# Shifting the moving tiles of a transformer block's matmuls by unused gaps in SBUF

## The chip, the cores and the metric

The kernel runs on one core of a Trainium2 chip. The metric is device time of one launch in microseconds; before the change the median of three runs is 1527.2 us. Everything said about single instructions comes from one profiled execution of the program.

## The reference

One encoder layer on 256 tokens of width 2048, in float32, with 256 memory tokens:

```python
h = rms_norm(x, norm_g[l, 0])
q, k, v, g, lr, u_f, u_h, u_s = jnp.split(h @ w_in[l], split_at, axis=-1)
...                                   # four mixers: gated linear attention, FFT, long and short convolution
x = x + mix @ w_out[l]
x = x + cross_attention(rms_norm(x, norm_g[l, 1]), mem_n, w_xq[l], w_xkv[l], w_xo[l])
x = x + swiglu(rms_norm(x, norm_g[l, 2]), w_gate_up[l], w_down[l])
return rms_norm(x, final_norm_g)
```

`cross_attention` has 4 heads of width 512: queries from the tokens, keys and values from the memory, softmax, output projection. `swiglu` is `(silu(h @ w_gate) * (h @ w_up)) @ w_down` with an inner width of 5632, which is 44 tiles of 128.

## The kernel before

Activations are held transposed: one tile `[128, 512]` per 128 features, with the high part of the 256 tokens in columns 0 to 255 and the low part (what the rounding to the matmul's type left over) in columns 256 to 511. Such tiles are `act0` to `act23`, `oex0` to `oex3` (attention output), `pt0` and `pt1` (transposed probabilities), `q`, `kt` (queries and transposed keys of a head) and `f0` to `f35` (SwiGLU). Values are kept as `vh` and `vl`, high and low part in tiles of their own.

All weights stream through the class `Stream`: `Stream._half` (L89, L90) takes 1024 columns of a loaded slab `raw`, casts them into `wh` on ScalarE and subtracts into `wl` on VectorE. There are three buffers of each, and up to the end of the attention one more pair from an extra pool. `Block.mm` (L262 to 272) multiplies one 128 x 128 block of weights, stationary, with one activation tile, moving: `wh` with all 512 columns (L269), `wl` with the 256 high columns (L270). That is a pair. In narrow places the first is split into two of 256 columns (L266, L267). `Block.gemm` runs `mm` over the reduction tiles `k` of each output column, one column after the other, except for a first group of four columns that are interleaved by parts. `gemm_rows` (L321 to L323) does it the other way round: activations stationary, weights moving.

The order of the stages in time: keys and values of the memory, the input projection with the four mixers, the output projection of the mixers, the queries of four heads with scores and probability-value products between them (`attention` and `head`), the attention's output projection, gate and up of the SwiGLU, down of the SwiGLU, the final norm. The queue of small steps between matmuls (`Background`) is filled while the program is recorded, by estimated costs of matmuls and VectorE work, and not by addresses.

`attention` opens three pools: `atp` for `oex`, `pt` and the scale `qs`; `kp` for `kt`, `q`, `vh`, `vl`; `mp` with five buffers `mr`, into which keys and values come back from DRAM through POOL's queue (L580). The output projection's moving tiles are

```python
o = act[0:8] + oex + act[8:12]
```

and in `mlp` the down projection's are

```python
f = act[4:12] + [fp.tile([P, 512], F32R, name=f"f{i}") for i in range(36)]
```

so 8 of its 44 reduction tiles are `act` tiles and 36 are `f` tiles. In `head`, `kt` moves over the stationary `q` (L637, L638), and `pt` over the stationary `vh` and `vl` (L664, L665).

Pools are laid out one behind the other in a partition, so the size of what lies ahead of a tile sets its address. The start addresses in bytes of a partition, as the built programs have them, and their remainders modulo 512 (all tiles of a kind have the same remainder, and so have all 128-column blocks of a weight tile):

| tiles | before | remainder | after | remainder |
|---|---|---|---|---|
| `act0`.. (moving) | 16512.. | 128 | 16512.. | 128 |
| `wh`, `wl` (stationary) | 128224.. | 224 | 128224.. | 224 |
| `f0`.. (moving over `wh`, `wl`) | 152800.. | 224 | 153216.. | 128 |
| `oex0`.. (moving over `wh`, `wl`) | 160992.. | 224 | 161408.. | 128 |
| `pt0`.. (moving over `vh`, `vl`) | 169184.. | 224 | 169600.. | 128 |
| `kt` (moving over `q`) | 173312.. | 256 | 173824.. | 256 |
| `q` (stationary) | 189696.. | 256 | 190304.. | 352 |
| `vh`, `vl` (stationary) | 206080.. | 256 | 207072.. | 224 |
| `mr` (landing place) | 222464.. | 256 | 223456.. | 224 |

Moving less stationary, modulo 512, is 416 for `act` over the weights in both programs; for `f` and `oex` over the weights 0 before and 416 after; for `kt` over `q` 0 and 416; for `pt` over `vh` and `vl` 480 and 416.

Of the kernel before, what the change touches and what calls it, by code (L numbers as in the profile page):

```python
# [13 lines left out]
F32 = mybir.dt.float32  # L14
F32R = mybir.dt.float32r
# [7 lines left out]
P = 128  # L23
# [126 lines left out]
class Block:  # L150
# [42 lines left out]
    def split2(self, hi, lo, src):  # L193
        self.nc.scalar.copy(hi, src)
        self.tt(lo, src, hi.bitcast(F32), ALU.subtract)

    def sumsq(self, acc, src, first):
        if first:
            self.nc.scalar.activation(acc, src, AF.Square)
        else:  # L200
            s = self.tmp()
            self.nc.scalar.activation(s, src, AF.Square)
            self.tt(acc, acc, s, ALU.add)
# [343 lines left out]
    def attention(self):  # L547
        tc, nc, act, st = self.tc, self.nc, self.act, self.st
        with tc.tile_pool(name="atp", bufs=1) as atp, tc.tile_pool(name="kp", bufs=1) as kp, \
                tc.tile_pool(name="mp", bufs=5) as mp:  # L550
            oex = [atp.tile([P, 512], F32R, name=f"oex{i}") for i in range(4)]
            pt = [atp.tile([P, 512], F32R, name=f"pt{i}") for i in range(2)]
            qs = atp.tile([P, 2], F32, name="qs")
            o = act[0:8] + oex + act[8:12]
            slot = lambda name, n: kp.tile([P, 512], F32R, name=name, tag=name, bufs=n)
            kv = [([], [], []) for _ in range(4)]

            def ev_q(q, p):
                q.append(slot("q", 8))
                self.split(q[-1], self.merge(p))  # L560

            def scales():

                col = self.rstd_begin([[self.acc]], D)
                nc.vector.tensor_scalar(out=qs, in0=col, scalar1=512 ** -0.5, scalar2=None, op0=ALU.mult)
                yield

            heads = []

            def load_kv():  # L570

                todo = [(hd, what, i) for hd in range(4) for what in range(2) for i in range(4)]
                parts = []

                def fetch():
                    if len(parts) < len(todo):
                        hd, what, i = todo[len(parts)]
                        m = mp.tile([P, R], F32, name="mr", tag="mr")
                        o = (4 * hd + i) * R
                        nc.gpsimd.dma_start(m, (self.vd if what else self.kd)[:, o:o + R])  # L580
                        parts.append(m)

                for _ in range(5):
                    fetch()
                yield 4
                for n, (hd, what, i) in enumerate(todo):
                    while hd > len(heads) + 1:
                        yield
                    if what == 0:
                        kv[hd][0].append(slot("kt", 8))  # L590
                        self.split(kv[hd][0][-1], parts[n])
                    else:
                        if i % 2 == 0:
                            kv[hd][1].append(slot("vh", 4))
                            kv[hd][2].append(slot("vl", 4))
                        c = slice(i % 2 * R, i % 2 * R + R)
                        self.split2(kv[hd][1][-1][:, c], kv[hd][2][-1][:, c], parts[n])
                    fetch()
                    yield 1.0

            def scores(hd, q):
                while len(kv[hd][2]) < 2:
                    yield
                yield
                yield from self.head(q, *kv[hd], pt, o[4 * hd:4 * hd + 4], qs)
                heads.append(hd)

            lp = [list(range(8)), list(range(8, 16))]
            self.bg.add(scales())
            self.bg.add(load_kv())  # L610
            gens = []
            for hd in range(4):
                q = []
                if hd > 1:
                    self.bg.drain(gens[hd - 2], True)
                self.gemm("w_xq", [(4 * hd + i) * P for i in range(4)], self.h2, lambda i, p: ev_q(q, p), first=(4, lp),
                          before=lambda n: n and hd == 0 and self.bg.drain(self.late))
                gens.append(self.bg.add(scores(hd, q)))
            h3 = self.h3 = act[12:24] + act[0:4]

            def ev_o(i, p):
                self.residual(i, p, V_NG + 32 + i, h3[i] if i < 12 else None)
                if i == 12:
                    st.extra = None

            self.gemm("w_xo", [i * P for i in range(16)], o,
                      ev_o,
                      first=(4, [list(range(12)), list(range(12, 16))]), before=lambda n: n == 1 and self.bg.drain())
            self.bg.add(self.rest(h3, 12, V_NG + 32))
# [41 lines left out]
    def mlp(self):  # L671
        tc, nc, act = self.tc, self.nc, self.act
        with tc.tile_pool(name="fp", bufs=1) as fp:
            f = act[4:12] + [fp.tile([P, 512], F32R, name=f"f{i}") for i in range(36)]
            box = {}

            def ev(i, p):
                u = self.merge(p)
                self.tt(u, u, box["rs"], ALU.mult)
                if i % 2 == 0:  # L680
                    nc.scalar.activation(u, u, AF.Silu)
                    box["g"] = u
                else:
                    self.tt(u, u, box["g"], ALU.mult)
                    self.split(f[i // 2], u)

            cols = []
            for j in range(FT):
                cols += [j * P, DFF + j * P]
            self.bg.add(self.rstd_later(self.acc, D, box))  # L690
            self.gemm("w_gate_up", cols, self.h3, ev, first=(4, [list(range(12)), list(range(12, 16))]),
                      before=lambda n: n and self.bg.drain())
            warm = self.tmp()[:, 0:1]
            nc.scalar.activation(warm, self.ones[:, 0:1], AF.Sqrt)
            last = self.tmp()

            def ev_down(i, p):
                x = self.resk(i)
                self.tt(x, x, p[:, 0:R] if i == 15 else self.merge(p), ALU.add)
                sq = last if i == 15 else self.acc if i == 0 else self.tmp()  # L700
                nc.scalar.activation(sq, x, AF.Square)
                if 0 < i < 15:
                    self.tt(self.acc, self.acc, sq, ALU.add)
                nc.scalar.activation(x, x, AF.Copy, scale=self.gvec(V_FG, i))

            self.gemm("w_down", [i * P for i in range(16)], f, ev_down,
                      first=(4, [list(range(40)), list(range(40, 44))]), narrow_last=True)

            p = self.bank()[:, 0:R]
            for i, a in enumerate((self.acc, last)):  # L710
                nc.tensor.matmul(p, self.ones, a, start=i == 0, stop=i == 1)
            v, y, a, rs = (self.tmp() for _ in range(4))
            nc.vector.tensor_scalar(out=v, in0=p, scalar1=1.0 / D, scalar2=EPS, op0=ALU.mult, op1=ALU.add)
            nc.scalar.activation(a, v, AF.Sqrt)
            nc.vector.reciprocal(y, a)
            self.stt(a, y, -0.5, y, ALU.mult, ALU.mult)
            self.tt(a, a, v, ALU.mult)
            self.stt(p, a, 1.5, y, ALU.add, ALU.mult)
            nc.scalar.copy(rs, p)
            for i in range(0, KT, 2):  # L720
                x = self.res[i // 4][:, i % 4:i % 4 + 2, :]
                if i in POOLS:
                    nc.gpsimd.tensor_tensor(out=x, in0=x, in1=rs.unsqueeze(1).to_broadcast([P, 2, R]), op=ALU.mult)
                else:
                    self.tt(x, x, p.unsqueeze(1).to_broadcast([P, 2, R]), ALU.mult)
                (nc.scalar if i % 4 else nc.sync).dma_start(self.t["out"][:, i * R:(i + 2) * R], x.rearrange("p k r -> p (k r)"))
# [513 lines left out]
```

## Time and profile before

| | |
|---|---|
| median of three runs | 1527.2 us (1527.15 to 1528.36) |
| the profiled execution | 1526.68 us, of which its span 1524.6 us |
| PE (matmul) busy | 1502.2 us, 99% of the span |
| VectorE, ScalarE busy | 995.5 us, 787.3 us |
| granted TensorE clock, mean | 0.995 |
| attention's output projection | about 679 to 772 us |
| gate and up | about 772 to 1262 us |
| down | about 1264 to 1509 us |

[...] A row of a group reads: line, engine, operation, written tile, read tiles (moving first, then stationary), shapes, count; busy time of the group and mean duration of one in ns; idle time of the engine ahead of it and what ended most of that. In the table of stages each row is a stretch in us, its length, and for PE, PEld, DVE, ACT and POOL the busy time and the number of instructions, then the granted clock, the share of the DMA engines and GB/s.

### The profile page before, as it was taken

To read this page: it belongs to the slowest core of one execution; us is meant where nothing else is said; L and a number is where in the kernel's file an instruction comes from. 1 tells how busy PE (TensorE), PEld (TensorE's weight loads), DVE (VectorE), ACT (ScalarE), POOL (GpSimd) and SP (SyncE) were. 2 spreads that over 40 slices of the span, in tenths; PEclk is the share of its full clock that TensorE was granted. 3 is DMA by queue.
4 is the path that set the end of the run, shared out by engine and by line. 5 is a ranking of instruction groups with operands and counts; after the bars stand their busy time and mean duration, and the time that the engine had idled before them with its cause. 6 is when DMAs were issued, how large, how long until landed. Compare 5 with 4: busy or idle time off the path is not lost.

```text
span 1524.6 us, 22257 instructions
## 1 busy us (share of the span) xinstructions
PE 1502.2 (99%) x8788; PEld 1311.2 (86%) x8788; DVE 995.5 (65%) x1532; ACT 787.3 (52%) x1238; POOL 40.0 (3%) x76
## 2 busy tenths in 40 slices
PE   8999999999999999999999999999999999999996
PEld 7887788889999788888888888888888888888885
DVE  6676668678667766867766666666666664555454
ACT  6664555557445655656554444444444444444442
POOL 0100100000002000100000000000000000000000
PEclk9999999999999999999999999999999999999998
DMA  9965554354346555544545555555555555555552
GB/s 353 343 239 190 198 193 166 139 195 159 139 167 241 195 190 182 177 149 166 194 166 193 189 185 185 189 192 194 193 193 186 186 186 190 192 192 180 183 191 83
DMA packets 48808, 290.53 MB, mean 191 GB/s; under 512 B 6173, under 2 KB 7486, under 8 KB 17088
## 3 DMA queue, kind: packets, MB, share of 16 engines
q1 hardware_dynamic: 44912, 279.59, 51.5%
q0 software_dynamic: 3072, 8.39, 1.6%
q8 instruction: 69, 1.13, 0.3%
q10 hardware_dynamic: 720, 1.13, 0.2%
q14 instruction: 35, 0.29, 0.0%
HBM read 282.80 MB, written 6.29 MB: 190 GB/s over the span
## 4 chain that ended last, share of the span: by engine, by line
PE 96%; DVE 1%; DMA 1%; issue 1%; ACT 0%; SPq 0%; POOL 0%; DVEq 0%; POOLq 0%; ACTq 0%
PE pg L269 49%; PE pg L270 28%; PE pg L266 3%; PE pg L267 3%; PE pg L321 3%; PE pg L323 2%; PE pg L322 2%; PE pm L269 1%; PE pm L796 1%; DMA mr<-values 1%; PE pm L664 1%; PE pm L270 0%; PE pm L637 0%; DMA raw<-in_W 0%; DVE wl L90 0%
## 5 line engine op out<-in xcount | busy, mean ns | idle before, releaser
L269 PE MATMUL pg<-act,wh 128*128 128x512 f32 x2680 | 939.7, 394 | 8.3 <-DVE act L182 4.5
L90 DVE TENSOR_TENSOR wl<-raw,wh 128x1024 fp32r<-128x1024 f32 (+1 forms) x507 | 617.0, 1218 | 425.9 <-ACT wh L89 423.6
L270 PE MATMUL pg<-act,wl 128*128 128x256 f32 x3008 | 842.5, 281 | 0.0
L89 ACT CAST wh<-raw 128x1024 fp32r<-128x1024 f32 (+1 forms) x507 | 529.5, 1046 | 589.5 <-PE pg L269 333.4
L269 PEld LDWEIGHTS pg<-act,wh 128*128 128x128 f32 x2680 | 504.7, 188 | 120.7 <-ACT wh L89 4.5
L270 PEld LDWEIGHTS pg<-act,wl 128*128 128x128 f32 x3008 | 566.9, 189 | 2.6 <-issue 2.0
L269 PE MATMUL pg<-f,wh 128*128 128x512 f32 x540 | 191.3, 398 | 0.0
L270 PE MATMUL pg<-f,wl 128*128 128x256 f32 x576 | 161.8, 281 | 0.0
L269 PEld LDWEIGHTS pg<-f,wh 128*128 128x128 f32 x540 | 101.5, 188 | 25.2
L270 PEld LDWEIGHTS pg<-f,wl 128*128 128x128 f32 x576 | 108.8, 189 | 0.0
L266 PE MATMUL pg<-act,wh 128*128 128x256 f32 x328 | 94.8, 289 | 0.0
L267 PE MATMUL pg<-act,wh 128*128 128x256 f32 x328 | 92.1, 281 | 0.0
L178 DVE TENSOR_TENSOR tmp<-pg,tmp 128x256 f32<-128x256 f32 x183 | 76.2, 417 | 5.7 <-ACT tmp L276 5.0
L276 ACT COPY tmp<-pg 128x256 f32<-128x256 f32 x179 | 65.0, 364 | 14.6 <-PE pg L270 14.5
L321 PE MATMUL pg<-wh,act 128*128 128x512 f32 x160 | 66.4, 415 | 0.0
L323 PE MATMUL pg<-wh,act 128*128 128x512 f32 x160 | 63.3, 395 | 0.0
L322 PE MATMUL pg<-wl,act 128*128 128x512 f32 x160 | 62.9, 393 | 0.0
L266 PEld LDWEIGHTS pg<-act,wh 128*128 128x128 f32 x328 | 61.9, 189 | 0.7
L267 PEld LDWEIGHTS pg<-act,wh 128*128 128x128 f32 x328 | 61.9, 189 | 0.3
L178 DVE TENSOR_TENSOR tmp<-tmp,rs 128x256 f32<-128x256 f32 x88 | 37.3, 425 | 2.9
L321 PEld LDWEIGHTS pg<-wh,act 128*128 128x128 f32 x160 | 30.0, 188 | 10.4 <-issue 2.9
L322 PEld LDWEIGHTS pg<-wl,act 128*128 128x128 f32 x160 | 30.1, 188 | 7.5 <-issue 1.0
(233 smaller groups left out, 985.1 us busy)
## 6 DMA issues: line engine op xcount, KB each, us to landing
raw<-in_W SPq DMA_DIRECT2D x247, 1024.0 KB, 4.8
raw<-in_W SPq DMA_DIRECT2D x9, 512.0 KB, 7.3
res<-in_xT SPq DMA_DIRECT2D x8, 512.0 KB, 5.6
k<-in_mem SPq DMA_DIRECT2D x8, 256.0 KB, 9.0
k<-in_x SPq DMA_DIRECT2D x8, 256.0 KB, 8.2
keys<-tmp POOLq DMA_DIRECT2D x16, 128.0 KB, 5.7
values<-tmp POOLq DMA_DIRECT2D x16, 128.0 KB, 2.4
mr<-keys POOLq DMA_DIRECT2D x16, 128.0 KB, 3.5
```

Of the source, the lines that this page charges most:

```text
L89: nc.scalar.copy(wh[:, a:b], r[:, a:b])
L90: nc.vector.tensor_tensor(out=wl[:, a:b], in0=r[:, a:b], in1=wh[:, a:b].bitcast(F32), op=ALU.subtract)
L178: self.nc.vector.tensor_tensor(out=out, in0=a, in1=b, op=op)
L266: self.nc.tensor.matmul(p[:, 0:R], wh, slot[:, 0:R], start=start, stop=False)
L267: self.nc.tensor.matmul(p[:, 0:R], wh, slot[:, R:512], start=False, stop=False)
L269: self.nc.tensor.matmul(p[:, :], wh, slot[:, :], start=start, stop=False)
L270: self.nc.tensor.matmul(p[:, 0:R], wl, slot[:, 0:R], start=False, stop=stop)
L276: self.nc.scalar.copy(t, p[:, R:512])
L321: nc.tensor.matmul(ps[r][:, :], hi, wh, start=k == 0, stop=False)
L322: nc.tensor.matmul(ps[r][:, :], hi, wl, start=False, stop=False)
L323: nc.tensor.matmul(ps[r][:, :], lo, wh, start=False, stop=k == nk - 1)
L664: nc.tensor.matmul(p[:, :], vh[m][:, s], pt[m][:, :], start=m == 0, stop=False)
```

## The change

Unused tiles ("gaps") go ahead of `oex`, `q`, `vh` and `f` in their pools, `q` and the values get pools of their own, and `qs` grows from 8 to 128 bytes, of which the instructions still use 8.

```diff
+    def gap(self, pool, n):
+
+        pool.tile([P, n // 4], F32, name=f"gap{next(self.kept)}")
...
         with tc.tile_pool(name="atp", bufs=1) as atp, tc.tile_pool(name="kp", bufs=1) as kp, \
+                tc.tile_pool(name="qp", bufs=1) as qp, tc.tile_pool(name="vp", bufs=1) as vp, \
                 tc.tile_pool(name="mp", bufs=5) as mp:
+            self.gap(atp, 416)
+            self.gap(qp, 96)
+            self.gap(vp, 384)
             oex = [atp.tile([P, 512], F32R, name=f"oex{i}") for i in range(4)]
             pt = [atp.tile([P, 512], F32R, name=f"pt{i}") for i in range(2)]
-            qs = atp.tile([P, 2], F32, name="qs")
+            qs = atp.tile([P, 32], F32, name="qs")[:, 0:2]
             o = act[0:8] + oex + act[8:12]
-            slot = lambda name, n: kp.tile([P, 512], F32R, name=name, tag=name, bufs=n)
+            slot = lambda name, n: dict(kt=kp, q=qp).get(name, vp).tile([P, 512], F32R, name=name, tag=name, bufs=n)
...
         with tc.tile_pool(name="fp", bufs=1) as fp:
+            self.gap(fp, 416)
             f = act[4:12] + [fp.tile([P, 512], F32R, name=f"f{i}") for i in range(36)]
```

## The prediction

> **What bounds the kernel now.** I read the page first, then the stages one by one, then the starts of single matmuls. Part 1 of the page, the chain that ended last and two rows of part 5:
>
> ```profile
> span 1524.6 us, 22257 instructions
> ...
> PE 1502.2 (99%) x8788; PEld 1311.2 (86%) x8788; DVE 995.5 (65%) x1532; ACT 787.3 (52%) x1238; POOL 40.0 (3%) x76
> ...
> PE 96%; DVE 1%; DMA 1%; issue 1%; ACT 0%; SPq 0%; POOL 0%; DVEq 0%; POOLq 0%; ACTq 0%
> ...
> L269 PE MATMUL pg<-act,wh 128*128 128x512 f32 x2680 | 939.7, 394 | 8.3 <-DVE act L182 4.5
> ...
> L269 PE MATMUL pg<-f,wh 128*128 128x512 f32 x540 | 191.3, 398 | 0.0
> ```
>
> TensorE is on 96% of the chain, so a nanosecond more or less on a matmul arrives at the end of the kernel. The last two rows are the same instruction on two kinds of moving tile, and `f` costs 4 ns more by the modelled durations. The starts say it better, because matmuls overlap. The table of stages, restricted to TensorE's stretches in the SwiGLU (gate and up, then down):
>
> ```profile
> 772.00:1262.00 490.00, 489.98 (x2828) 431.24 (x2828) 318.51 (x456) 238.30 (x356) 0.00 (x0) 1.00 0.53 189
> 1262.00:1512.00 250.00, 248.93 (x1455) 217.94 (x1454) 123.90 (x136) 109.86 (x138) 0.00 (x0) 1.00 0.48 173
> ```
>
> The second number is PE busy. In gate and up, 2828 matmuls are 1414 pairs (`wh` with 512 columns, `wl` with 256) in 490.0 us: 346.5 ns a pair, all of them on `act` tiles. The clock is 1.00 in both stages, VectorE is busy 65% and 50%. Now one output column of the down projection, which goes through 8 `act` tiles and then 36 `f` tiles; start, duration, instruction:
>
> ```profile
> 1400.94 0.39 PE L269 MATMUL pg<-act,wh 128*128 128x512 f32 x1
> ...
> 1403.72 0.40 PE L269 MATMUL pg<-f,wh 128*128 128x512 f32 x1
> ...
> 1416.42 0.39 PE L269 MATMUL pg<-act,wh 128*128 128x512 f32 x1
> ```
>
> Eight pairs on `act` take 2.78 us, 347 ns each; 36 pairs on `f` take 12.70 us, 353 ns each. Same stage, same weights, same shapes, no waits. One by one the `f` pairs repeat 350, 361, 349 ns from start to start; the `act` pairs stand at 346 to 348 within two or three pairs after them. What differs is the address of the moving tile. `act` lies at remainder 128 modulo 512 and the weights `wh`, `wl` at 224, so `act` is 416 bytes past them; `f` lies at 224, 0 past. The output projection of the attention reads 12 `act` and 4 `oex` tiles (`oex` also at 224), and the scores read `kt` over `q`, both at 256:
>
> ```profile
> L269 PE MATMUL pg<-act,wh 128*128 128x512 f32 x186 | 65.5, 393 | 0.0
> ...
> L269 PE MATMUL pg<-oex,wh 128*128 128x512 f32 x64 | 23.3, 398 | 0.0
> ...
> L637 PE MATMUL pm<-kt,q 128*128 128x512 f32 x8 | 2.9, 398 | 0.0
> ```
>
> That is the group view from 679 to 772 us. `oex` pairs are at 350 to 361 ns where `act` pairs are at 347, and the last head's scores show the same cycle of 350, 361, 349. So wherever the moving tile lies 0 past the stationary one, the cycle can appear; heads 0 and 1 of the scores, also at 0, settle at 347, so 0 allows the slow cycle rather than forces it.
>
> **The change part by part.** In the built programs each engine issues the same instructions in the same order with the same semaphore waits; only addresses differ, and the row length of `qs`. Nothing is added to an engine or a queue. After the change `f`, `oex` and `pt` lie at 128, `q` at 352, `vh`, `vl` and `mr` at 224; `kt` stays at 256. Every pair of moving and stationary is then 416 apart, except the projections that hold `act` stationary and stream the weights (96, untouched).
>
> *`f`, down projection.* The 540 pairs exceed 346.8 ns each by 3.3 us together (15 columns of 12.70 - 36 x 0.3468 = 0.215 us give 3.2). The nearest row for what they become is `act` in the same columns, at the same remainder: 346.8 ns. Bounds: 346 and 361 ns, the fastest and the slowest pair seen, so from 3.7 us saved to 4.4 us lost (540 x 8.2 ns); I take 346.8, as 1409 pairs in gate and up average that. The last column is narrow, three matmuls of 256 columns a tile: 108 steps at 119.9 ns on `f` against 118.75 on `act`, 0.1 us.
>
> *`oex`.* 63 measured pairs exceed 346.8 by 0.3 us, and the `act` pairs that follow them, which carry the cycle for a few pairs, by another 0.25. Together 0.55 us.
>
> *Scores and `pt`.* 64 pairs. The scores exceed 346.8 ns by about 0.1 us without their waits; the probability-value product (480 apart today) has mostly 347 and some 361, 0.1 us. Some of the latter sits beside waits of PE for `pt`, so I count 0.15, with ends 0 and 0.25.
>
> *`qs`, the gaps.* A gap tile is never written. `qs` grows from 2 to 32 columns, but the instructions still touch 2. Casts and subtractions into `f` write at 128 instead of 224; the casts take 406 ns into `act` (at 128) and 399 into `f` (at 224), the subtractions 418 into both, and PE waits for neither in this stage, so nothing.
>
> *What would be late next.* The down projection takes a half slab of weights per 8 pairs: 2.78 us instead of 2.82. The supply needs 1.05 us of ScalarE and 1.22 of VectorE per half, and gate and up already runs at 2.77 with more evacuation beside it. So it holds.
>
> Sum: 3.3 + 0.1 + 0.55 + 0.15 = 4.1 us. The profiled execution took 1526.68 us, of which the span is 1524.62; it lies 0.5 us below the median of the runs, 1527.2. It would become 1522.6, and the median 1523.1.
>
> [...]
>
> **The rivals.** *It is the place, not the offset.* `act` lies at bytes 16,512 to 65,664 of a partition, the weights at 128,224 to 160,992, `f` and `oex` from 152,800 up. If high tiles are slow to stream, shifting them by 416 bytes changes nothing: 1527.2. For it: no high tile at 416 exists in this trace. Against it: `pt`, from 169,184, streams mostly at 347 ns a pair at offset 480, and heads 0 and 1 of the scores, from 173,312, at 347, while `oex` beside `pt` cycles.
>
> *The change does not do what it says.* It does: the addresses above are those of the changed program. What stays open is only whether they matter.
>
> *Slower: the fetch of keys and values.* PE's longest stop after the start is here:
>
> ```profile
> 498.94 0.79 PE L269 MATMUL pg<-act,wh 128*128 128x512 f32 x1 [3.73 <-DVE tmp L178]
> ```
> ```profile
> 495.94 0.40 ACT L194 CAST vh<-mr 128x256 fp32r<-128x256 f32 x1 [3.02 <-DMA mr<-values]
> ```
> ```profile
> 499.00:504.50 5.50, 5.50 (x17) 0.51 0.73 262
> ```
>
> ScalarE stands 3.02 us before the cast of `vh` until the transfer into `mr` lands, the next weight cast stands behind it, and PE idles 3.73 us. The granted clock is then 0.51 for 5.5 us: seven pairs at 0.64 us instead of 0.347, 2.05 us more. The `mr` tiles move from remainder 256 to 224. Two landings of 4.6 us lie on the chain before the stop. If they lengthened, PE would stop longer by twice that. To end slower than before by over 0.2% they must lengthen by (4.1 + 3.05) / 2 = 3.6 us each, 78%, giving 1530.3 or more. Against: `raw` already lands at remainder 224 and takes 1024 KB in 4.8 us. The same place can also move the other way: two landings shorter by 1 us each give 2 us and, if the clock then stays up, another 2.05: about 1519.
>
> **How the numbers follow.** The 4.1 us saved: 0.79. No effect of the offset: 0.12. Slower by the fetch: 0.05. The stop at 498.94 shortens as well: 0.04. 0.2% of the time, about what a measurement of this kernel can tell from no change, is 3.05 us, so the forecast clears it by 1.0 us; the three runs lie 1.2 us apart, and I give a tenth of the first case to "within". Faster 0.79 x 0.9 + 0.04 = 0.75; same 0.08 + 0.12 = 0.20; slower 0.05. The likeliest case alone spans 1522.2 to 1524.4. The range reaches down to a slightly shorter stop, 1521.4, and up towards the case without effect, 1526.6.
>
> **What would show it.** Right: in the changed profile the `f` row reads 392 ns like `act` in that stage, one column of 36 `f` pairs takes 12.48 us instead of 12.70, the down projection's PE stretch is 3.4 us shorter, gate and up and everything before 476 us is unchanged, and `oex` is at 347 ns a pair. Wrong: the `f` pairs still cycle through 350, 361, 349 (the place decides), or the difference sits around 480 to 505 us (the fetch decides). If `f` is at 347 and the time hardly moves, the stop at 498.94 has grown.

## The result, and the profile after

| | before | after |
|---|---|---|
| median of nine runs each | 1527.79 us (1526.0 to 1528.36) | 1523.4 us (1521.86 to 1524.58) |
| the profiled execution | 1526.68 us, span 1524.6 | 1523.47 us, span 1521.4 |

The ratio of after to before is 0.9971, with a 95% interval of 0.9961 to 0.9982: 4.4 us less, by more than the 0.2% that can be told from no change. A later series of eight runs gave 0.9973 (0.9962 to 0.9983).

The page of the changed kernel, part 1 and the two rows of part 5 that stood in the prediction. The diff shifts the lines of the file, so L269 is now L273 and L270 is L274:

```profile
span 1521.4 us, 22257 instructions
...
PE 1498.4 (98%) x8788; PEld 1310.7 (86%) x8788; DVE 995.8 (65%) x1532; ACT 787.3 (52%) x1238; POOL 40.0 (3%) x76
...
L273 PE MATMUL pg<-act,wh 128*128 128x512 f32 x2680 | 939.6, 394 | 9.3 <-ACT wh L89 4.9
...
L273 PE MATMUL pg<-f,wh 128*128 128x512 f32 x540 | 187.9, 392 | 0.0
```

The `act` row is what it was; the `f` row fell from 398 to 392 ns. PE busy fell by 3.8 us. By stages (stretch, length, then busy us and count for PE, PEld, VectorE, ScalarE and POOL, then clock, DMA share, GB/s):

```profile
772.00:1262.00 490.00, 489.98 (x2827) 431.24 (x2827) 319.23 (x457) 237.97 (x355) 0.00 (x0) 1.00 0.54 189
1262.00:1512.00 250.00, 245.74 (x1458) 217.56 (x1457) 126.61 (x140) 110.56 (x138) 0.00 (x0) 1.00 0.49 173
```

Gate and up is unchanged to one matmul; the down projection has 245.7 us of work where it had 248.9. The same kind of output column as before, 8 `act` tiles and then 36 `f` tiles:

```profile
1399.44 0.39 PE L273 MATMUL pg<-act,wh 128*128 128x512 f32 x1
...
1402.21 0.39 PE L273 MATMUL pg<-f,wh 128*128 128x512 f32 x1
...
1414.69 0.39 PE L273 MATMUL pg<-act,wh 128*128 128x512 f32 x1
```

The 36 `f` pairs take 12.48 us, 346.7 ns each, where they took 12.70. The two matmuls of a pair last 0.39 and 0.28 us in the profile, 0.67 together, so they overlap, and the starts are what is compared. From start to start all 540 `f` pairs of the trace are at 346 or 347 ns; the cycle of 350, 361 and 349 is gone. In the attention's output projection the groups now read

```profile
L273 PE MATMUL pg<-act,wh 128*128 128x512 f32 x191 | 66.9, 392 | 0.0
...
L273 PE MATMUL pg<-oex,wh 128*128 128x512 f32 x60 | 21.7, 393 | 0.0
```

where `oex` stood at 398. One row went the other way. The stop of PE near 499 us is longer than before, 4.42 us instead of 3.73, with ScalarE standing before a cast of `vh` as before and with the same slow clock after it:

```profile
500.21 0.79 PE L273 MATMUL pg<-act,wh 128*128 128x512 f32 x1 [4.42 <-DVE tmp L178]
```
```profile
497.21 0.40 ACT L194 CAST vh<-mr 128x256 fp32r<-128x256 f32 x1 [3.04 <-DMA mr<-values]
```
```profile
500.00:506.00 6.00, 5.79 (x18) 0.51 0.70 255
```

By the profile, what PE waits for last there is not the weights but the sum on VectorE (`tmp`, L178) that empties a tile of matmul results (`pg`). The copy on ScalarE that this sum needs comes out of the same queue, at 499.08 us, behind the same casts (497.21 and 498.47).

The traces can be lined up at fixed instructions, here the first score matmul and the last two matmuls of the program, before and after:

```profile
599.69 0.39 PE L637 MATMUL pm<-kt,q 128*128 128x512 f32 x1
...
1510.76 0.70 PE L711 MATMUL pm<-tmp,ones 128*128 128x256 f32 x2 [0.53 <-ACT tmp L701]
```
```profile
601.01 0.40 PE L645 MATMUL pm<-kt,q 128*128 128x512 f32 x1
...
1507.57 0.70 PE L720 MATMUL pm<-tmp,ones 128*128 128x256 f32 x2 [0.53 <-ACT tmp L710]
```

Up to the first score matmul 1.3 us are lost: 0.59 in the first 11 us of the program, where nothing was moved, and 0.75 at the stop. From it to the last matmul's end it is 911.77 us before and 907.26 after, 4.51 us less: 0.10 in the queries and scores, 0.63 in the attention's output projection, 0.02 in gate and up, 3.75 in the down projection.

### The profile page after: what moved, and what is told of

It is laid out like the page before. It is cut to its first block, busy times and chain, and to the rows that moved or that the text cites. A ratio compares the mean times of both kernels' runs of the same rounds, so it can differ in the third digit from the quotient of the medians.

```text
span 1521.4 us, 22257 instructions
## 1 busy us (share of the span) xinstructions
PE 1498.4 (98%) x8788; PEld 1310.7 (86%) x8788; DVE 995.8 (65%) x1532; ACT 787.3 (52%) x1238; POOL 40.0 (3%) x76
## 4 chain that ended last, share of the span: by engine, by line
PE 96%; DVE 1%; DMA 1%; issue 1%; ACT 0%; POOL 0%; DVEq 0%; SPq 0%; POOLq 0%
PE pg L273 49%; PE pg L274 28%; PE pg L270 3%; PE pg L271 3%; PE pg L325 3%; PE pg L327 2%; PE pg L326 2%; PE pm L273 1%; PE pm L805 1%; PE pm L274 1%; DMA mr<-values 1%; PE pm L672 1%; PE pm L645 0%; DVE wl L90 0%; PE pm L646 0%
## 5 line engine op out<-in xcount | busy, mean ns | idle before, releaser
L273 PE MATMUL pg<-act,wh 128*128 128x512 f32 x2680 | 939.6, 394 | 9.3 <-ACT wh L89 4.9
L274 PE MATMUL pg<-act,wl 128*128 128x256 f32 x3008 | 842.4, 280 | 0.0
L273 PEld LDWEIGHTS pg<-act,wh 128*128 128x128 f32 x2680 | 504.8, 188 | 121.5 <-ACT wh L89 4.9
L274 PEld LDWEIGHTS pg<-act,wl 128*128 128x128 f32 x3008 | 566.7, 188 | 2.6 <-issue 2.0
L273 PE MATMUL pg<-f,wh 128*128 128x512 f32 x540 | 187.9, 392 | 0.0
L274 PE MATMUL pg<-f,wl 128*128 128x256 f32 x576 | 161.0, 280 | 0.0
L273 PEld LDWEIGHTS pg<-f,wh 128*128 128x128 f32 x540 | 101.3, 188 | 22.4
L274 PEld LDWEIGHTS pg<-f,wl 128*128 128x128 f32 x576 | 108.2, 188 | 0.0
L270 PE MATMUL pg<-act,wh 128*128 128x256 f32 x328 | 94.8, 289 | 0.0
L178 DVE TENSOR_TENSOR tmp<-pg,tmp 128x256 f32<-128x256 f32 x183 | 76.3, 418 | 5.1 <-ACT tmp L280 4.5
L270 PEld LDWEIGHTS pg<-act,wh 128*128 128x128 f32 x328 | 61.9, 189 | 0.7
L178 DVE TENSOR_TENSOR tmp<-tmp,rs 128x256 f32<-128x256 f32 x88 | 37.3, 425 | 2.9
```

Of the source, the lines that this page charges most:

```text
L178: self.nc.vector.tensor_tensor(out=out, in0=a, in1=b, op=op)
L270: self.nc.tensor.matmul(p[:, 0:R], wh, slot[:, 0:R], start=start, stop=False)
L273: self.nc.tensor.matmul(p[:, :], wh, slot[:, :], start=start, stop=False)
L274: self.nc.tensor.matmul(p[:, 0:R], wl, slot[:, 0:R], start=False, stop=stop)
```

## The experiments

The theory: with the moving tile at some distances from the stationary one, modulo a power of two, the pair of matmuls falls into a slower cycle; 416 is free of it and 0 is not. The rivals: the place of `f` in the partition decides; only that something was moved counts; the gain came through the transfers into `mr`.

### All offsets inside one kernel

```diff
-            self.gap(fp, 416)
-            f = act[4:12] + [fp.tile([P, 512], F32R, name=f"f{i}") for i in range(36)]
+            f = act[4:12]
+            for g, ahead in enumerate((0, 64, 64, 64, 64, 64, 64, 64, 480)):
+                if ahead:
+                    self.gap(fp, ahead)
+                f += [fp.tile([P, 512], F32R, name=f"f{4 * g + i}") for i in range(4)]
```

> The changed kernel, but the 36 f tiles lie in nine groups of four at offsets 0, 64, 128, 192, 256, 320, 384, 448 and 416 bytes past the weights modulo 512. Theory of the offset: the pairs on the group at 416 take 347 ns from start to start, those on the group at 0 take 350 to 361, and the others show which offsets are free; next to 0 (448, 64) is where I expect the slow cycle to reach, if it reaches anywhere. Rival (the act of moving the tiles out of their old place, at any offset, is what helped): all nine groups at the same time per pair. Span between the two kernels, 1521 to 1525 us.

The second kernel has the gaps `(32, 64, 64, 64, 64, 64, 64, 64, 32)`.

> The same with the offsets in between: 32, 96, 160, 224, 288, 352, 416, 480 and 0. Theory of the offset: 416 at 347 ns, 0 at 350 to 361, 480 mostly 347 with some 361 (as the probability-value product, which lay at 480 before the change, shows), 32 like 480 if the effect is symmetric about 0. Rival (only moving helped): all the same.

One execution each: 1524.91 and 1524.27 us, with the kernel before at a median of 1526.81 on the same chip. The starts in the two traces, tile by tile over the 15 wide columns, give these pairs in ns (the four tiles of a group in their order; each value repeats within 1 ns from column to column, and a group's first pairs also depend on the group ahead of it). The last group of each kernel is left out of the table, since what stands ahead of it weighs on it: 353, 349, 347, 347 at 416 and 359, 349, 347, 347 at 0.

| offset | pairs | mean | offset | pairs | mean |
|---|---|---|---|---|---|
| 0 | 342, 350, 361, 349 | 351 | 256 | 346, 348, 361, 349 | 351 |
| 32 | 348, 347, 347, 347 | 347 | 288 | 343, 353, 346, 347 | 347 |
| 64 | 345, 357, 355, 348 | 351 | 320 | 345, 357, 355, 348 | 351 |
| 96 | 347, 347, 388, 348 | 358 | 352 | 347, 347, 388, 348 | 358 |
| 128 | 349, 343, 356, 348 | 349 | 384 | 349, 343, 356, 348 | 349 |
| 160 | 348, 347, 346, 347 | 347 | 416 | 348, 347, 347, 347 | 347 |
| 192 | 354, 347, 353, 353 | 352 | 448 | 354, 348, 353, 353 | 352 |
| 224 | 350, 352, 343, 361 | 351 | 480 | 350, 352, 343, 361 | 351 |

Every group from 64 on repeats itself 256 bytes further on, within 1 ns. So the remainder modulo 512 was more than was needed; modulo 256 is enough here. And the offsets whose groups average 347 ns are 32, 160, 288 and 416, that is 32 modulo 128. That only the move counted is excluded: of the fifteen offsets other than 0, eleven average 349 to 358 ns. My own guess that 480 and 32 would be alike was wrong.

The groups are short, so a slow group can owe something to the change from one offset to the next, and the second kernel's last group, at 0 behind 480, ran at 347 after its first pairs while 0 in the first kernel cycled. So two offsets were given to all 36 tiles:

```diff
-            self.gap(fp, 416)
+            self.gap(fp, 32)
```

> The changed kernel with f at 32 past the weights instead of 416, all 36 tiles. Theory that the offset counts modulo 128 and that 32 is the free remainder (416 = 3 x 128 + 32, and the groups at 32, 160, 288 and 416 of the two sweeps run at 346.5 to 348 ns): f pairs at 346.7 ns, the down projection as long as in the changed kernel, 245 us. Rival (416 modulo 512 itself is needed, the groups of four in the sweep were too short to settle): f pairs above 349 ns, 1.3 us or more.

and the same with 96:

> The changed kernel with f at 96 past the weights, all 36 tiles. In the sweep one pair in four took 388 ns at 96 and at 352, the others 347. Theory modulo 128: 96 is not free, pairs between 350 and 357 ns on average, 1.8 to 5.6 us more than the changed kernel; f could then be worse than at its old place (353). Rival (the 388 ns are the transition between two groups, not the offset): 346.7 ns after the first pairs of each column.

One execution each: 1523.38 and 1524.66 us, before at 1527.4. The down projection's row (stretch, length, PE busy, clock, DMA share, GB/s) with 32 and with 96:

```profile
1262.00:1512.00 250.00, 245.61 (x1457) 1.00 0.48 173
```
```profile
1262.00:1512.00 250.00, 246.98 (x1453) 1.00 0.48 173
```

At 32 the `f` pairs are at 346.7 ns on average, as at 416. At 96 they settle into an alternation of 349.5 and 350.5, 350.1 on average: not free, but better than the 353.0 of offset 0. The 388 of the sweep was the change from one group to the next, as the rival of that run said; that 96 is slow was not.

### Low tiles at offset 0

```diff
         wp = pool("wp", 3)
+        wp.tile([P, 104], F32, name="gapw", tag="gapw", bufs=1)
```

This is the kernel before with the weights shifted to where `act` lies, modulo 512.

> The kernel before with one gap of 416 bytes ahead of the weight buffers: wh and wl come to remainder 128, where act lies, so that low tiles too are at offset 0, and f and oex with them. Theory of the offset: the slow cycle appears on act tiles as well; if every one of the some 3100 pairs on act fell into it, 6.2 ns each, 19 us more than before (1546); since heads 0 and 1 of the scores settled at 347 ns at offset 0, part of the stretches may stay at 347, so between 1529 and 1546. Rival (it is the place of f in the partition, low tiles are fast at any offset): act pairs stay at 347 ns and the time is that of the kernel before, 1527 to 1528.

Median 1538.99 us of nine runs, ratio 1.0063 (1.0041 to 1.0085). Seven runs lie between 1538.1 and 1540.8, two at 1527.3 and 1528.0. In the profiled run, 1539.51 us, the stretch of gate and up, all on `act` tiles, got through 53 matmuls fewer than before (2775 instead of 2828) in the same 490 us, at the same clock:

```profile
772.00:1262.00 490.00, 490.00 (x2775) 424.77 (x2774) 313.80 (x451) 234.62 (x350) 0.00 (x0) 1.00 0.52 186
```

Its pairs average 353.3 ns where they were at 346.7. So `act`, the low tiles, cycle just as `f` does once they are 0 past the weights: the place is not the cause. In this kernel `f` lies at 153216, remainder 128, as in the changed kernel, and cycles all the same (1431 matmuls from 1262 to 1512 us, PE busy throughout at a clock of 1.00, against 1458 in 245.74 us of work in the changed kernel; since gate and up ends later here, the stretch is not quite the same work), so the tile's own address is not it either; what differs is the distance.

At offset 0 the cycle is one of two states, and this one trace shows both. In the input projection its `act` pairs average 353.3 ns from 195 to 240 us and 346.9 ns from 240 to 285 us, at the same offset and at a granted clock of 1.00; the turn at 240 us comes where other matmuls stand between the pairs. Heads 0 and 1 of the scores, at offset 0 in both kernels, settled at 347 before the change and cycle here. The two runs some 11 us below the others would fit a program that stays out of the cycle in gate and up, which takes 9.2 us longer here than before. They were not profiled, so that is not shown.

### Each part of the change alone

`f` alone: the gap in `mlp` only, everything of the attention as before.

> Of the change only the gap ahead of f: attention's tiles lie where they lay before. Theory of the offset: the f pairs go from 353.0 to 346.7 ns (3.4 us) and the narrow column gains 0.3 us, so 3.7 us less than before, 1524.1 where before is 1527.8; the attention's output projection stays at 350 to 361 ns on oex. If the attention part carried more of the gain than its 0.8 us, this one gains under 3 us.

1522.48 us against 1526.81, ratio 0.9971 (0.9959 to 0.9982). From the first score matmul to the last matmul's end it gains 3.76 us, all of it in the down projection, and the `oex` row still has its 398 ns:

```profile
1262.00:1512.00 250.00, 245.09 (x1455) 1.00 0.48 173
```
```profile
L273 PE MATMUL pg<-oex,wh 128*128 128x512 f32 x60 | 21.9, 398 | 0.0
```

The attention alone: everything but the gap in `mlp`.

> Of the change only the attention part: oex, pt, q, vh, vl and mr as in the changed kernel, f back at offset 0. Theory of the offset: oex and the scores go to 347 ns, 0.7 to 0.8 us less than before, f stays in the cycle of 350, 361 and 349 ns; 1526.0 where before is 1526.8, which the interval will hardly tell from no change. Rival (the attention part does more than its pairs, through the place where mr lands): over 2 us either way, and the stop of PE near 499 us clearly shorter or longer than the 3.7 to 4.6 us of the runs so far.

1527.19 us against 1527.4, ratio 0.9998 (0.9990 to 1.0007). Its trace has `oex` at 393 and the down projection's `f` pairs at 352.9 ns. From the first score to the first `f` matmul it saves 0.71 us; the interval holds that and no change alike. The stop of PE is 4.82 us here, 4.55 with `f` alone, where `mr` lies as before.

### The stop near 500 us

What blurs all of these is the stop of PE: 3.7 to 5.4 us in the kernels so far. Three kernels change what leads to it.

```diff
                     fetch()
-                    yield 1.0
+                    yield 2.0
```

> The changed kernel with keys and values taken from mr every 2.0 us of recorded matmul time instead of every 1.0 us. Theory (ScalarE stands before a cast of vh whose transfer has not landed, the weight cast behind it is late, PE stops 4.4 us and runs at a granted clock of 0.5 for some 5 us after it): with twice the time for each transfer ScalarE no longer waits for mr, PE does not stop near 500 us, and the kernel gains 4.4 + 2 = 6.4 us, to about 1516.5 where the changed kernel is at 1523. Rival (the stop comes from the start of the output projection itself): PE still stops 4 us near 500 and the time is that of the changed kernel.

1523.12 us, ratio to before 0.9976 (0.9965 to 0.9986): that of the changed kernel. The stop is there, 4.37 us at 499.39. The interval only orders the recording; in the finished program ScalarE's casts of `mr` still stand where they stood, early in the mixers' output projection: the first starts at 483.51 us, in the changed kernel at 484.60.

Then the transfers themselves were held back:

```diff
                         m = mp.tile([P, R], F32, name="mr", tag="mr")
+                        n = len(parts) - 5
+                        if 0 <= n < 11:
+                            nc.gpsimd.tensor_copy(m[:, 0:1], self.h2[n * 8 // 11][:, 0:1].bitcast(F32))
```

> The changed kernel, with the sixth to sixteenth transfer into mr each held back on POOL until one of the first eight columns of the mixers' output projection is in h2 (a copy of one column of h2 into mr ahead of the transfer, which the transfer overwrites). Theory (the stop of PE near 500 us comes from ScalarE standing before casts of mr while weight casts queue behind): the transfers come one per 3 to 6 us instead of in two bursts, ScalarE's waits for mr are each shorter than the two to three halves of weights that PE has ahead, the stop of 4.4 us and the 2 us of the slow clock behind it go; about 1517 where the changed kernel is at 1523.4. Rival (as with the longer interval, only the place of the stop moves): a stop of 3 us or more somewhere between 480 and 600 us, and the time of the changed kernel.

and, on the same chip,

> The changed kernel once more, beside the gated one on the same chip: 0.997 of the kernel before, the stop near 500 us between 3.7 and 5.2 us as in all runs so far.

1522.98 and 1523.02 us, ratios 0.9968 (0.9956 to 0.9981) and 0.9973. The rival was right: there is no stop at 500 us, but one of 3.32 us at 526.93. Two transfers waited for one column, and ScalarE stood before their cast:

```profile
525.20 0.73 ACT L194 CAST vh<-mr 128x256 fp32r<-128x256 f32 x2 [6.95 <-DMA mr<-values]
```

So it seems to be the cast's place in ScalarE's queue that counts. The third kernel holds back the casts. The transfers come one by one here as well (at 495.62, 497.11, 498.82, 501.69 us and so on), because from the sixth on each waits for a buffer that an earlier cast and its subtraction free:

```diff
+                def pace(n, first):
+                    nc.gpsimd.tensor_copy(first, self.resk(n * 14 // 16)[:, 0:1])
...
                         kv[hd][0].append(slot("kt", 8))
+                        if n < 16:
+                            pace(n, kv[hd][0][-1][:, 0:1])
...
                         c = slice(i % 2 * R, i % 2 * R + R)
+                        if n < 16:
+                            pace(n, kv[hd][1][-1][:, i % 2 * R:i % 2 * R + 1])
```

> The changed kernel, with each of the first sixteen casts of mr (heads 0 and 1) held back instead of the transfers: POOL first copies one element per partition of a finished column of the mixers' output projection into the kt or vh tile that the cast then overwrites, so that the casts of kt and vh stand in ScalarE's queue one per column, after their transfers have landed. Theory (PE stops because ScalarE stands before a cast whose transfer is still under way while weight casts queue behind it): no stop of PE over 1 us between 480 and 600 us, no stretch at a granted clock of 0.5, 4.4 + 2 us less than the changed kernel: 1516.5 where that is at 1523.0. Rival (the stop only moves again, as in the kernel with gated transfers): a stop of 3 us or more between 480 and 600 us and 1523.

1515.67 us against 1527.16, ratio 0.9928 (0.9915 to 0.9942), and the five runs lie within 0.5 us. PE has no stop between 480 and 600 us. The rows of 479 to 499 and 499 to 504.5 us, in the kernel before and in this one (stretch, length, PE busy, clock, DMA share, GB/s):

```profile
479.00:499.00 20.00, 16.27 (x95) 0.97 0.69 243
499.00:504.50 5.50, 5.50 (x17) 0.51 0.73 262
```
```profile
479.00:499.00 20.00, 20.00 (x117) 1.00 0.64 221
499.00:504.50 5.50, 5.50 (x33) 1.00 0.76 262
```

From 476 to 600 us ScalarE now stands 0.5 us in all before the casts of `kt` and 0.5 us before those of `vh`.

That is 7.3 us below the changed kernel's 1523.02, which was measured on another chip, instead of the 6.4 expected; by the ratios to the kernel before on each chip it is 6.9. Between the traces of the changed and the paced kernel, lined up at fixed matmuls, 7.27 us go between 495 and 507 us. In the trace of the changed kernel the stop is 4.42 us, and nine pairs after it take 5.80 us (500.21 to 506.01) instead of 3.12: 7.1 us in all. I had sized the slow stretch by seven pairs. The kernel before has nine slow pairs too, 5.73 us.

With this stop gone, the gaps can be weighed by themselves: the paced kernel with every tile back at its old address.

> The paced kernel without the gaps: every tile at its old address, f and oex at offset 0. It has no stop near 500 us, whose length scatters the other kernels by a microsecond either way, so it weighs the gaps alone. Theory of the offset: 4.1 to 4.4 us above the paced kernel, 1519.8 to 1520.1 where that is at 1515.7, and f back in the cycle of 350, 361 and 349 ns. Rival (the gaps gained less, and part of the gain measured so far was scatter of the stop): 1518 or less.

1520.72 us, ratio 0.9955 (0.9942 to 0.9969). There is no stop here either, and the `f` pairs are back at 353.0 ns. The gaps are worth 5.05 us between the two medians, a little above the 4.1 to 4.4 expected, but these come from two chips; by the ratios to the kernel before on each chip it is 4.1. In the two traces, from the first score matmul to the last matmul's end, it is 911.94 and 907.43 us: 4.51 us, the same as between before and after. The spans of the two profiled executions lie 5.7 us apart, and the rest of that, 1.2 us, is in the first 14 us of the program, ahead of every tile that the gaps move. Between other profiled executions the start differs too, by 0.6 us before and after the change and by 1.0 between the changed and the paced kernel, so half a microsecond between two medians says nothing about the gaps.

## Why the prediction was right

The forecast was 1523.1 us with 4.1 us saved; measured were 1523.4 and 4.4 us. The mechanism is the one forecast. That the totals agree within 0.3 us is partly luck: the runs of one kernel scatter by 2 to 3 us, and the two profiled executions, before and after, differ by 3.2. The steps:

- *PE is the path, so what a pair gains arrives at the end.* Right: 4.51 us in the trace from the scores on, against 4.1 summed.
- *`f` at 346.8 ns, 3.3 us.* Right: 346.7, and 3.4 us by the pairs. The slow bound, 361, did not occur at 416; with 32 and 96 for all 36 tiles the averages were 346.7 and 350.1.
- *The narrow column, 0.1 us.* Too small. Its steps went from 120.0 to 117.3 ns, below the 118.75 of `act` that I had taken as the floor. The `act` steps of that column fell to 117.3 as well, though no `act` tile was moved: what runs ahead of them weighs on them too. It is 0.3 us.
- *`oex`, 0.55 us; scores and `pt`, 0.15.* Measured 0.63 and 0.10.
- *It is the place, not the offset (0.12).* Excluded: `f`, a high tile, runs at 347, and low tiles cycle at offset 0.
- *Slower by the fetch (0.05).* It did not decide, but the stop grew by 0.7 us in the profiled execution. The landings into `mr` have medians of 3.1 and 3.3 us after the change and 3.5 and 4.2 before. The two of the chain went from 4.63 and 4.61 us to 3.19 and 4.65, while the first five, which the chain starts from, went from 4.2 to 5.2 us up to 6.2 to 6.7. The remainder alone does not set that: with `mr` at 256 the first five take 5.11 to 5.99 us with `f` alone and 5.55 to 6.25 in the paced kernel without the gaps; with `mr` at 224 they take 4.90 to 5.55 in the paced kernel. The stop is 3.73 and 4.55 us in the two kernels with `mr` at 256 whose casts were left alone, and 4.4 to 5.4 in the eight with `mr` at 224. Two against eight do not settle whether the new remainder lengthens it by some tenths.
- *Everything before 476 us unchanged.* True from 11 us on; the first 11 us took 0.59 us longer, in a stretch that the change does not touch.

In gate and up, the same instructions at the same granted clock of 1.00 take 346.7 ns a pair at offset 416 and 353.3 at offset 0, with the weights moved by 416 bytes against the tiles.

What goes on inside is not shown. The runs show that the distance of the two operands sets which cycles are possible (all 36 `f` tiles at 0, 96, 32 and 416: 353.0, 350.1, 346.7 and 346.7 ns), and that at offset 0 a cycle, once entered, can go on through tiles and columns, all of gate and up among them (353.3 ns on average over 490 us). They show neither why that is nor what decides between the two states.

## What to carry to other kernels

Where matmuls follow each other without a wait, compare the starts of equal pairs on different tiles: a few ns that differ by tile and not by shape can come from addresses, as they did here (347 against 353 ns), and a gap ahead of a pool is a cheap trial. For these float32r pairs (512 and 256 columns on 128 x 128 weights) distances of 416 and 32 bytes between moving and stationary, given to all 36 `f` tiles, ran at 346.7 ns, and 0 and 96 did not; of the others only groups of four were run. Then look for the larger thing beside it: here one stop of PE, in which ScalarE's queue stood before a cast whose transfer had not landed, cost 7.1 us, more than all the offsets (4.5 us in the traces), and blurred them by its scatter (3.7 to 5.4 us).

## What the runs showed of the hardware

- The same pairs at the same distance can run at two speeds. With all tiles at offset 0, one trace has `act` pairs at 353.3 ns from 195 to 240 us and at 346.9 from 240 to 285; and seven runs of that kernel lie near 1539 us, two near 1528.
- A pair settles at 346.7 ns at 32 and 416, although single pairs of 342 and 343 ns appear inside the slow cycles. What sets 346.7 was not looked for.
- A stop of PE of 4.42 us cost 7.1 us in the changed kernel, since the nine pairs after it took 0.64 us each on average instead of 0.35, with a granted clock of 0.51. The slow stretch did not grow with the stop: after 5.41 us, in the first kernel with all offsets, five pairs were slow, after 3.73, in the kernel before, nine.
